# Diffusion block on one core: the first four token tiles of x loaded behind all sixteen pieces of the modulation weights

## The chip, the cores and the metric

The kernel runs on one core of one Trainium2 chip. The metric is the device time of one execution in microseconds (us). A difference of about 0.3% (4 us here) is what a measurement of this kernel can tell from no change.

## What is computed

One layer of a generator over 1024 latent tokens of width 1024, with 256 context tokens of the same width, all in float32:

```python
def layer(x, ctx, c, c_ctx, ...):
    sh1, sc1, gt1, sh2, sc2, gt2 = modulation(c, w_mod, b_mod)      # silu(c) @ w_mod + b_mod
    csh1, csc1, ... = modulation(c_ctx, w_mod, b_mod)
    hx = rms_norm(x, g_pre_mix) * (1 + sc1) + sh1
    hc = rms_norm(ctx, g_pre_mix) * (1 + csc1) + csh1
    s_f, s_b = context_states(hc, w_in, conv_qkv, a_log, dt_bias)    # K, V columns and gates only
    yx, _, _ = token_mixers(hx, rows, s_f, s_b, ...)                 # in-projection, short conv,
    x = x + gt1 * rms_norm(yx, g_post_mix)                           # gated delta rule, pooling, out-projection
    hx = rms_norm(x, g_pre_ffn) * (1 + sc2) + sh2
    x = x + gt2 * rms_norm(conv_glu_ffn(hx, w_up, conv_ffn, w_down), g_post_ffn)
```

The change lies in the first forty microseconds: the shift and scale of the modulation, the norms of x and of the context, and the loads behind them.

## The kernel before

**The start.** The modulation needs w_mod's first 2048 columns (the shift and the scale) before any token can be modulated. `stream_mod` loads them as sixteen pieces of 512 KB (tile `w_mod`, `NW` = 5 buffers), four pieces for each group of 512 columns in the order 2, 3, 0, 1, so that the scale comes first. Each piece takes four matmuls of 128x512 into `pa`. After the fourth piece of a group ScalarE copies the result (`rows`), and eight small matmuls turn it into columns (`m`); VectorE adds the bias (`mod`) and forms the scale `a`. When the last group is through, the event M1 lets the modulation of tokens begin. A piece's buffer is free for the piece five later once its matmuls are done.

**The token tiles.** x comes in eight tiles of 128 tokens, 512 KB each (tile `xv`, six buffers, shared with the two tiles of the context). Tiles 0 to 3 make up the half X0, tiles 4 to 7 the half X1. `XLOAD` says behind which piece of the modulation each of the first four is issued on SP's queue, which issues in order. Tiles 4 to 7 and the first pieces of w_in for the context (`w_c`, which use the buffers of `w_mod`) follow in the list `POST`.

**The chains.** For each set of tiles ScalarE takes the squares (`sq`), VectorE the reciprocal root in nine small steps (`ssq`, `rs_h`, `rs_a`, `rstd`), VectorE and POOL scale the tiles (`xv<-xv,rstd`), TensorE transposes them, and the result is copied to `xT_C` or `xT_X`. After M1 a unit of work for each of eight slices k makes `h` (VectorE; for X1 ScalarE straight from the transposes), rounds it to `c_hi` or `h_hi`, and takes the rest `c_lo` or `h_lo` (POOL for odd k, VectorE for even k). The products are made of three matmuls: hi by hi, lo by hi, hi by lo. The weights are split in the same way: `w_hi` by ScalarE, `w_lo` by POOL for the context, by VectorE for x.

**The jobs.** `gemm_T` runs 28 jobs, each 128 columns of w_in. Jobs 0 to 7 are those of the context (24 matmuls of 256 columns; four give `kc`, four `vc`). The job after them, job 8, is the first of x: two halves of 24 matmuls of 512 columns, the first of X0 and the second of X1. Each result (`rawc`, `raw`) goes through a short convolution of four VectorE steps for the context, of 128x256 each (on `kc`, `vc`), or four of 128x1024 for x (on `cv`). `gate_mm` makes the gates' columns, and `gate_tables` the tables for the context (`gtmp` of 128x16) and then for x (`gtmp` of 128x64): a row of some seventeen small VectorE steps, then three small matmuls `pb<-gtmp`. The rest of the modulation's weights comes in 32 pairs `w_m` with two buffers through `mod_rest`, between the jobs.

**What sets the order.** `Streams.run` picks the next step by priority and by a planner's clock (`Clock`), which gives each instruction a time of its own reckoning. Every engine then runs its own queue in that order. So a load that is issued later in the plan moves the work behind it on all engines. An instruction that waits in an engine's queue holds up all that stands behind it there.

The two places at which the table is used:

```python
NW, XLOAD = 5, (5, 7, 9, 11)
...
            wl.append(w)
            for t, n in enumerate(XLOAD):
                if n == i:
                    load_x(0, t)
                    signal(f"x{t}")
```

Of the kernel before, what the change touches and what calls it, by code (L numbers as in the profile page):

```python
# [28 lines left out]
GR = T // GW  # L29
EPS = 1e-6  # L30
NBIG, NK, NT4 = 9, 4, 2
NW, XLOAD = 5, (5, 7, 9, 11)
PT4 = (3,)
POST = [("w", 0)] + [("x", t) for t in range(4, 8)] + [("w", j) for j in range(1, 5)]

# [1925 lines left out]
```

## Time and profile before

| what | us |
|---|---|
| median of three runs (lowest, highest) | 1355.26 (1353.31, 1358.17) |
| the profiled execution | 1355.82 |
| its span, first to last instruction | 1354.1 |
| TensorE busy, of the span | 1268.3 |
| VectorE, ScalarE, POOL busy | 987.1, 632.8, 343.4 |
| stage from 630 us to the end: TensorE busy | 705.83 of 724 |

TensorE is busy through nearly all of the second half (the feed-forward part) and has its gaps before, most of them in the first 120 us. A busy time says nothing of a wait inside an instruction: a VectorE instruction that is held up by POOL is listed as busy. Times of the profile are counted from the span's start.

### The profile page before, as it was taken

How to read it: one execution, taken by the hardware profiler on the slowest of the kernel's cores; microseconds unless marked ns; L12 is line 12 of the kernel's file. 1: busy time of each engine (PE TensorE's matmuls, PEld its weight loads, DVE VectorE, ACT ScalarE, POOL GpSimd, SP SyncE). 2: the span in 40 equal slices, each digit the busy share in tenths (PEclk: the TensorE clock that was granted, in tenths of full speed). 3: DMA queues.
4: the chain of work that ended last, by engine and by line, in shares of the span. 5: the costliest groups of instructions: out<-in, count | busy, mean ns of one | idle time of the engine just before them, and what ended most of it. 6: DMA issues, size and time to landing. Idle time of an engine off the chain costs nothing.

```text
span 1354.1 us, 23855 instructions
## 1 busy us (share of the span) xinstructions
PE 1268.3 (94%) x8655; PEld 1003.1 (74%) x8655; DVE 987.1 (73%) x1917; ACT 632.8 (47%) x1502; POOL 343.4 (25%) x431
## 2 busy tenths in 40 slices
PE   5888989898999799988998999999999999999997
PEld 1456668686878678856876788888888887888886
DVE  1876655666778788447769999999877878765673
ACT  3555856355676435345544333333333335544541
POOL 0552334141141510003012334433333320000122
PEclk9989989999999889988999999999999999999999
DMA  9513655545562323375322566666334348976561
GB/s 349 196 40 106 201 167 140 173 123 169 147 188 80 75 78 96 105 253 173 138 83 88 196 241 233 240 237 233 137 116 140 126 138 282 308 235 194 190 215 62
DMA packets 145301, 226.54 MB, mean 167 GB/s; under 512 B 53440, under 2 KB 66592, under 8 KB 142368
## 3 DMA queue, kind: packets, MB, share of 16 engines
q1 hardware_dynamic: 144752, 224.61, 50.3%
q8 instruction: 68, 1.11, 0.3%
q10 hardware_dynamic: 432, 0.42, 0.1%
q14 instruction: 49, 0.40, 0.1%
HBM read 164.77 MB, written 60.21 MB: 166 GB/s over the span
## 4 chain that ended last, share of the span: by engine, by line
PE 73%; DVE 10%; DMA 8%; POOL 3%; ACT 3%; issue 2%; SPq 1%; DVEq 0%; POOLq 0%; ACTq 0%
PE pc L123 25%; PE pa L123 25%; PE pb L123 22%; DMA w_mod<-in_wmod 2%; POOL stmp L123 2%; POOL sX L123 1%; DVE hf L123 1%; DMA mx<-mixd 1%; DMA w_m<-in_wmod 1%; DVE gtmp L123 1%; DMA sc<-blk_x 1%; SPq L123 1%; DMA wo_st<-in_w_out 1%; DVE wql L123 1%; DMA sB<-blk_i 1%
## 5 line engine op out<-in xcount | busy, mean ns | idle before, releaser
L123 POOL TENSOR_TENSOR a<-a,a 128x512 f32<-128x512 f32 x88 | 149.7, 1702 | 315.6 <-DVE wql L123 142.3
L123 ACT CAST wqh<-a 128x512 fp32r<-128x512 f32 x132 | 80.8, 621 | 162.9 <-PE pb L123 73.3
L123 DVE TENSOR_TENSOR op<-dst,op 128x512 fp32r<-128x512 f32 x154 | 103.8, 714 | 57.4 <-ACT op L123 56.9
L123 PE MATMUL pa<-h_hi,w_hi 128*128 128x512 f32 x320 | 138.5, 433 | 2.5 <-ACT jk L123 1.2
L123 ACT CAST op<-dst 128x512 fp32r<-128x512 f32 x154 | 90.0, 620 | 93.8 <-PE pc L123 32.2
L123 PE MATMUL pa<-h_hi,w_lo 128*128 128x512 f32 x320 | 129.8, 406 | 1.6 <-DVE w_lo L123 1.6
L123 PE MATMUL pa<-h_lo,w_hi 128*128 128x512 f32 x320 | 130.1, 407 | 0.0
L123 PE MATMUL pc<-op 128*128 128x512 f32 x528 | 121.5, 390 | 0.0
L123 DVE TENSOR_TENSOR wql<-a,wqh 128x512 fp32r<-128x512 f32 x132 | 104.8, 796 | 18.4 <-ACT wqh L123 18.0
L123 PEld LDWEIGHTS pc<-op 128*128 128x128 f32 x528 | 99.0, 188 | 21.7 <-DVE graw L123 0.5
L123 DVE TENSOR_TENSOR hf<-hf 128x512 f32<-128x512 f32 (+1 forms) x109 | 92.0, 850 | 8.1 <-ACT hf L123 6.9
L123 POOL TENSOR_TENSOR hf<-hf,gg 128x512 f32<-128x512 f32 x16 | 21.3, 1350 | 214.5 <-ACT t L123 214.5
L123 PEld LDWEIGHTS pa<-h_hi,w_hi 128*128 128x128 f32 x320 | 61.2, 191 | 16.1 <-issue 2.8
L123 PEld LDWEIGHTS pa<-h_hi,w_lo 128*128 128x128 f32 x320 | 60.9, 190 | 13.9 <-DVE w_lo L123 1.8
L123 DVE SCALAR_TENSOR_TENSOR cv<-raw,sm,cv 128x1024 f32<-128x1024 f32 x48 | 62.5, 1301 | 11.4 <-ACT cv L123 10.8
L123 DVE SCALAR_TENSOR_TENSOR hf<-graw,sm,hf 128x1024 f32<-128x1024 f32 x44 | 70.0, 1590 | 0.7
L123 PEld LDWEIGHTS pa<-h_lo,w_hi 128*128 128x128 f32 x320 | 61.4, 192 | 9.6 <-issue 2.0
L123 ACT ACTIVATE hf<-hf 128x1024 f32<-128x1024 f32 x22 | 23.3, 1061 | 58.7 <-DVE hf L123 58.7
L123 PE MATMUL pa<-op 128*128 128x512 f32 x198 | 50.4, 390 | 0.0
L123 PE MATMUL pb<-op 128*128 128x512 f32 x198 | 50.3, 389 | 0.0
L123 ACT ACTIVATE ws<-pc,btg 128x128 f32<-128x128 f32 x80 | 26.8, 367 | 48.1 <-PE pc L123 47.7
L123 DVE TENSOR_TENSOR w_lo<-w_st,w_hi 128x512 fp32r<-128x512 f32 x40 | 28.4, 713 | 26.5 <-ACT w_hi L123 16.3
(388 smaller groups left out, 3328.0 us busy)
## 6 DMA issues: line engine op xcount, KB each, us to landing
a<-in_w_up_t SPq DMA_DIRECT2D x90, 256.0 KB, 3.2
w_m<-in_wmod SPq DMA_DIRECT2D x64, 256.0 KB, 3.2
hf<-in_w_down SPq DMA_DIRECT2D x22, 512.0 KB, 4.3
td<-hf SPq DMA_DIRECT2D x11, 1024.0 KB, 4.7
gd<-hf SPq DMA_DIRECT2D x22, 512.0 KB, 2.6
sd<-hf SPq DMA_DIRECT2D x11, 1024.0 KB, 5.4
dst<-sd SPq DMA_DIRECT2D x44, 256.0 KB, 4.7
dst<-td SPq DMA_DIRECT2D x44, 256.0 KB, 4.5
```

The lines of the kernel that those rows point to most:

```text
L123: return f(*a, **k)
```

## The change

The four numbers of `XLOAD` become 15 each: the loads of tiles 0 to 3 of x are issued behind the last of the sixteen pieces, all four together, instead of behind pieces 5, 7, 9 and 11.

```diff
-NW, XLOAD = 5, (5, 7, 9, 11)
+NW, XLOAD = 5, (15, 15, 15, 15)
```

**First place: the modulation.** SP's queue at the start, with the loads of the context's tiles, of w_mod's pieces and of x's tiles; before is -, now is +:

```order
 L123 DMA xv<-in_ctx 128x1024 x2
-L123 DMA w_mod<-in_wmod 128x1024 x6
-L123 DMA xv<-in_x 128x1024
-L123 DMA w_mod<-in_wmod 128x1024 x2
-L123 DMA xv<-in_x 128x1024
-L123 DMA w_mod<-in_wmod 128x1024 x2
-L123 DMA xv<-in_x 128x1024
-L123 DMA w_mod<-in_wmod 128x1024 x2
-L123 DMA xv<-in_x 128x1024
-L123 DMA w_mod<-in_wmod 128x1024 x4
+L123 DMA w_mod<-in_wmod 128x1024 x16
+L123 DMA xv<-in_x 128x1024 x4
```

The four tiles stand behind all pieces; ten loads of pieces move ahead of one or more of them. TensorE's queue from the last but one group of pieces to the context's gates (`pb<-cst,xv` are transposes of x's tiles):

```order
 L123 MATMUL m_186<-cst,rows 128x2 x4
-L123 MATMUL pa<-w_mod,cs 32x512 x4
-L123 MATMUL pb<-cst,xv 128x128 x6
-L123 MATMUL pa<-w_mod,cs 32x512 x2
-L123 MATMUL pb<-cst,xv 128x128 x2
-L123 MATMUL pa<-w_mod,cs 32x512 x2
-L123 MATMUL pb<-cst,xv 128x128 x5
+L123 MATMUL pa<-w_mod,cs 32x512 x8
 L123 MATMUL m_186<-cst,rows 128x2 x4
-L123 MATMUL pb<-cst,xv 128x128 x11
 L123 MATMUL pc<-c_hi_144,wg 32x256
 L123 MATMUL pc<-c_hi_145,wg 32x256
```

No transpose of x stands between the last pieces any more.

**Second place: x's first half behind the context.** POOL's queue (`c_lo` and `w_lo` belong to the context, `xv` to X0, `h_lo` to X0's slices):

```order
 L123 ISA
-L123 TENSOR_SCALAR xv<-xv,rstd 128x1024 x3
+L123 TENSOR_SCALAR xv<-xv,rstd 128x1024
+L123 TENSOR_TENSOR c_lo_153<-h_369,c_hi_145 128x256
+L123 TENSOR_TENSOR c_lo_155<-h_380,c_hi_147 128x256
+L123 TENSOR_TENSOR c_lo_157<-h_384,c_hi_149 128x256
+L123 TENSOR_TENSOR c_lo_159<-h_398,c_hi_151 128x256
+L123 TENSOR_TENSOR w_lo<-w_c,w_hi 128x512 x2
+L123 TENSOR_SCALAR xv<-xv,rstd 128x1024 x2
+L123 TENSOR_TENSOR w_lo<-w_c,w_hi 128x512 x6
+L123 TENSOR_TENSOR h_lo_128<-h_596,h_hi_120 128x512
```

POOL scales two tiles of X0 behind the context's four `c_lo` and job 0's two `w_lo`, and goes on with six `w_lo`. TensorE's queue in job 1, now:

```order
 L123 MATMUL pa<-c_hi_148,w_hi 128x256
 L123 MATMUL pa<-c_lo_156,w_hi 128x256
+L123 MATMUL pb<-gtmp_180,cst 128x8 x2
+L123 MATMUL pb<-gtmp_180,cst 128x16
+L123 MATMUL pb<-cst,xv 128x128 x4
+L123 MATMUL pa<-c_hi_148,w_lo 128x256
+L123 MATMUL pa<-c_hi_149,w_hi 128x256
+L123 MATMUL pa<-c_lo_157,w_hi 128x256
```

The first transposes of X0 stand behind the matmuls of the context's gate table.

**Third place: the gate tables of x.** TensorE's queue in job 8, before, where `pb<-gtmp_180` are the matmuls on that table:

```order
 L123 MATMUL pa<-c_hi_151,w_lo 128x256
-L123 MATMUL pa<-h_hi_119,w_hi 128x512
-L123 MATMUL pa<-h_lo_127,w_hi 128x512
-L123 MATMUL pa<-cst,kc 128x128 x3
-L123 MATMUL pa<-h_hi_119,w_lo 128x512
-L123 MATMUL pb<-gtmp_180,cst 128x32 x2
-L123 MATMUL pb<-gtmp_180,cst 128x64
```

They stand behind three matmuls of job 8's first half. Now, where `pa<-cst,kc` ends the first half:

```order
 L123 MATMUL pa<-cst,kc 128x128 x4
+L123 MATMUL pa<-h_hi_119,w_hi 128x512
+L123 MATMUL pa<-h_lo_127,w_hi 128x512
+L123 MATMUL pa<-h_hi_119,w_lo 128x512
+L123 MATMUL pa<-h_hi_120,w_hi 128x512
+L123 MATMUL pa<-h_lo_128,w_hi 128x512
+L123 MATMUL pa<-h_hi_120,w_lo 128x512
+L123 MATMUL pb<-gtmp_180,cst 128x32 x2
+L123 MATMUL pb<-gtmp_180,cst 128x64
```

Thirty matmuls of job 8, the first half and six of the second, stand ahead of the first matmul on x's gate table.

## Rows read from the trace of the kernel before

**Rows 1.** The page: busy us of each engine, share, instructions.

```profile
PE 1268.3 (94%) x8655; PEld 1003.1 (74%) x8655; DVE 987.1 (73%) x1917; ACT 632.8 (47%) x1502; POOL 343.4 (25%) x431
```

**Rows 2.** Stages: window, length, busy us of each engine, PEclk, DMA share, GB/s.

```profile
10.00:20.00 10.00, 9.73 (x46) 3.60 (x48) 4.05 (x17) 1.69 (x4) 1.60 (x1) 1.00 0.95 352
...
59.50:73.10 13.60, 7.57 (x35) 3.69 (x33) 13.40 (x40) 6.73 (x14) 8.40 (x6) 0.82 0.25 81
73.10:97.00 23.90, 20.32 (x117) 11.88 (x116) 19.74 (x31) 10.62 (x21) 17.67 (x13) 0.89 0.01 2
...
630.00:1354.00 724.00, 705.83 (x3087) 574.47 (x3085) 572.80 (x814) 290.28 (x522) 171.59 (x147) 1.00 0.53 182
```

**Rows 3.** Timeline, the end of the modulation: start, us, instruction, [idle before, releaser].

```profile
30.24 1.05 PE L123 MATMUL pa<-w_mod,cs 128*32 128x512 f32 x4 [0.17 <-DMA w_mod<-in_wmod]
...
34.01 0.14 PEld L123 LDWEIGHTS pa<-w_mod,cs 128*32 128x32 f32 x4 [0.91 <-DMA w_mod<-in_wmod]
...
38.21 1.92 PE L123 MATMUL pa<-w_mod,cs 128*32 128x512 f32 x4
...
40.69 1.19 PE L123 MATMUL pa<-w_mod,cs 128*32 128x512 f32 x4
...
43.65 0.17 DVE L123 TENSOR_TENSOR mod<-m,sm 128x16 f32<-128x16 f32 x1 [0.46 <-PE m L123]
```

**Rows 4.** Waits of SP's queue to 60 us: total us, times, longest.

```profile
SPq L123 <- PE pa L123: 9.6, 10, 2.0
```

**Rows 5.** Timeline, ScalarE and VectorE on X0 and the context.

```profile
27.82 1.06 ACT L123 ACTIVATE sq<-xv 128x1024 bf16<-128x1024 f32 x1 [2.31 <-DMA xv<-in_x]
...
33.00 0.17 DVE L123 TENSOR_SCALAR ssq<-ssq 128x4 f32<-128x4 f32 x1 [7.01 <-ACT sq L123]
...
40.58 0.69 DVE L123 COPY xT_X<-pb 128x512 f32<-128x512 f32 x1 [3.04 <-PE pb L123]
...
45.04 1.02 ACT L123 CAST c_hi<-h 128x256 fp32r<-128x256 f32 x3
```

**Rows 6.** Timeline of VectorE beside POOL's work.

```profile
55.31 0.55 DVE L123 TENSOR_SCALAR h<-xT_X,a,mod 128x512 f32<-128x512 f32 x1
...
63.55 1.29 DVE L123 TENSOR_TENSOR gtmp<-gtmp,gtmp 128x16 f32<-128x16 f32 x1
64.76 0.68 DVE L123 TENSOR_TENSOR h_lo<-h,h_hi 128x512 fp32r<-128x512 f32 x1
...
66.53 0.47 DVE L123 SCALAR_TENSOR_TENSOR kc<-rawc,sm,kc 128x256 f32<-128x256 f32 x1
...
72.87 0.16 DVE L123 SCALAR_TENSOR_TENSOR rstd<-rs_a,rstd 128x4 f32<-128x4 f32 x1
```

**Rows 7.** Timeline of POOL.

```profile
63.51 3.06 POOL L123 TENSOR_TENSOR w_lo<-w_c,w_hi 128x512 fp32r<-128x512 f32 x2 [0.17 <-ACT w_hi L123]
...
73.13 4.90 POOL L123 TENSOR_SCALAR xv<-xv,rstd 128x1024 f32<-128x1024 f32 x4 [1.20 <-DVE rstd L123]
...
94.44 1.45 POOL L123 TENSOR_TENSOR h_lo<-h,h_hi 128x512 fp32r<-128x512 f32 x1 [1.43 <-DVE h_hi L123]
```

**Rows 8.** Timelines of ScalarE and VectorE at x's gate table.

```profile
97.03 0.59 ACT L123 COPY gx<-pc 128x512 f32<-128x512 f32 x1 [4.47 <-PE pc L123]
...
114.33 0.21 DVE L123 TENSOR_TENSOR gtmp<-gtmp,gv 128x64 f32<-128x64 f32 x1
```

**Rows 9.** Timeline of TensorE: first and last matmul of job 8, a wait behind it.

```profile
110.10 0.40 PE L123 MATMUL pa<-h_hi,w_hi 128*128 128x512 f32 x1
...
130.59 0.39 PE L123 MATMUL pa<-h_hi,w_lo 128*128 128x512 f32 x1
...
137.96 0.43 PE L123 MATMUL pb<-w_m,cs 128*32 128x128 f32 x8 [0.59 <-DMA w_m<-in_wmod]
```

**Rows 10.** The page's DMA issues: count, KB, us from issue to landing.

```profile
w_m<-in_wmod SPq DMA_DIRECT2D x64, 256.0 KB, 3.2
```

## The prediction, made before the change was run

> **What bounds the kernel now.** I read the busy times first [rows 1]: TensorE works 1268 of 1354 us. The stages [rows 2] say where it doesn't: from 630 us on it is busy 705.8 of 724 us, so nothing at the start is worth anything there except by arriving sooner. From 59.5 to 73.1 us it works 7.6 of 13.6 us, VectorE 13.4. So the first 120 us are bound by VectorE and by POOL beside it, and the question is how soon TensorE can run the jobs of x. The first of these, job 8, begins at 110.1 and ends at 130.8 [rows 9]; behind it TensorE is nearly full. I take the end of job 8 as the mark: what the change moves there I carry to the end, since every later step hangs on earlier ones and not on a time of day.
>
> VectorE's prices, from starts of neighbouring rows (a row overlaps the next by some 0.08 us): `h` of 512 columns 0.46, `h_lo` 0.60, a convolution step 0.40, a copy `xT_X` 0.69, a small step 0.17 to 0.20 [rows 5, 6]. POOL's: `w_lo` 1.3 to 1.5, a tile `xv` 1.22, `h_lo` 1.45 [rows 7]. The two engines hinder each other: a `gtmp` step on 16 columns took 1.29 us beside a `w_lo` [rows 6, 7]. To price that I count VectorE's own work in a stage and ask which share of POOL's time is added. From 47.6 to 73.1 us VectorE had some 16.2 us of own work and POOL 15; the stage took 25.5, a share of 0.62. From 73.1 to 97.0 it had 10.9 (12 convolution steps, 8 roundings of about 0.36, 4 `h_lo`), POOL 17.7, and the stage took 23.9 [rows 2], a share of 0.7. These shares hold the waits for other engines too.
>
> **The change, step by step.**
>
> *M1 sooner.* Pieces 11 and 13 were used at 30.24 and 34.01 as they landed; between them came two pieces and a tile of x, 1.26 us each [rows 3]. Piece 15 would land at 34.0 + 2 x 1.26 = 36.5, but TensorE took pieces 14 and 15 at 38.21 and 40.69, since transposes of X0 stood ahead of them. With four loads of 512 KB taken out of the way piece 15 lands 4 x 1.26 = 5.0 us sooner, at 31.5 (30.6 at the 352 GB/s of 10 to 20 us [rows 2]), with no transposes between. From the last matmul to the end of `mod` is 43.84 - 40.69 = 3.2 us. M1 comes at 34.7 instead of 43.84: 9.1 us gained for the context. If it isn't the transfers that pace the pieces but SP's waits for buffers, 9.6 us in ten waits [rows 4], up to 4 us of this is lost.
>
> *X0's root later.* Tile 3 lands behind piece 15, at 31.5 + 5.0 = 36.5. ScalarE now has four `sq` (1.15 with the accumulator's read) and eight `c_hi` (0.35) in one queue [rows 5], 7.4 us from the first `h` at 35.05, with waits of some 0.5 for VectorE: X0's `ssq` comes at 42.9, against 33.0.
>
> *X0's transposes much later.* VectorE then has nine steps of the root (1.8), seventeen of the context's table (2.9), two tiles (1.5) and job 0's four convolution steps (1.6): 7.8 us. POOL has seven `w_lo` and two tiles, 11.7 us, times 0.62 is 7.3. That gives 58.0; TensorE takes the table's matmuls and, behind them, the first transposes of X0, with its clock likely low after the wait: 60.5, against 40.6 for the first copy before [rows 5]. This is the change's price, 20 us on X0, while job 0 and what hangs on it are sooner. The ends: 54 if the seventeen steps slip through between POOL's instructions, 65 if each of POOL's costs its full time.
>
> *X0's slices.* From 60.5: four copies (2.8), eight `h` (3.7), four `h_lo` (2.4), eight convolution steps (3.2), the root of X1 and small steps (2.9), 15.0 us; POOL five `w_lo` and four `h_lo`, 12.3 times 0.62 is 7.6. X1's root is ready at 83.1, against 73.0 [rows 6]. Tiles 6 and 7 wait for the buffers of tiles 0 and 1, so for X0's last transpose, near 72; they have 10 us for the load and two `sq`, which is enough but no more.
>
> *X1's slices.* Before, 73.0 to 95.9 (the last `h_lo` [rows 7]): 22.9 us with twelve convolution steps. Now again twelve, four of `kc` and eight of `vc`, and one `w_lo` less on POOL, 0.9: 22.0 us. X1 is ready at 105.1, 9.2 us later than before.
>
> *From X1 to the end of job 8.* Before, 130.8 - 95.9 = 34.9 us: four jobs of the context were still to come, with sixteen steps on `vc` and four `w_lo` of POOL, and x's gate table stood ahead of job 8. From the copy `gx` at 97.03 to the table's last product with `gv` at 114.5 [rows 8] went 17.5 us. Now eight steps on `vc` and all `w_lo` of the context are behind us: 17.5 less 4 x 1.4 x 0.7 = 3.9 and about 1 for a silu of `kc` that came earlier is 12.6, so the table is ready 1.1 + 12.6 = 13.7 us after X1. TensorE fills that time with 28 matmuls of the context (0.12 each) and 30 of job 8 (0.23), 10.3 us. It then has 18 matmuls (4.1) and three groups of `w_m` (1.4), and meets one wait for a pair of `w_m` of some 1.5 (a pair takes 3.2 us to land and has two buffers [rows 10]). Sum 20.7 us: job 8 ends at 125.8, 5.0 us sooner.
>
> *Behind job 8.* Two pairs of `w_m` now stand between jobs 9 and 10 with only twelve transposes and a few small matmuls between them, 2.4 us, against 3.2 for the landing: 0.8 us lost, of the kind of the 0.59 at 137.96 [rows 9].
>
> Sum: +9.2 at X1 (the 9.1 of M1 are already in it, eaten by X0's delay), -14.2 from there to the end of job 8, +0.8 behind it: -4.2 us. The profiled execution took 1355.82 us, 0.56 above the median of 1355.26; carried to the median the forecast is 1351.1.
>
> **The rivals.**
>
> *Slower: POOL holds VectorE for its full time.* The `gtmp` row of 1.29 us [rows 6] shows a small step that waited for all of a `w_lo`. If every instruction of POOL in the three stages costs VectorE its whole time, the shares 0.62 and 0.7 become 1: 0.38 x (11.7 + 12.3) + 0.3 x 16 = 13.9 us more, 1365. It decides from 4.2 us, a share of about 0.73 in all three. For it: POOL's work now comes in rows, nine instructions back to back behind the context; against: before had such rows too, and they are in the shares. The Trainium skill, "SBUF — State Buffer", section "Who interferes with whom", states that a VectorE instruction of this kind and a POOL instruction that reads the buffer exclude each other for the whole instruction; by that rule this rival's sum is the right one. The trace agrees for the `gtmp` row, but the shares over a stage are lower, since copies from PSUM and waits for others fall beside POOL's work.
>
> *No change: the lead on TensorE is given back.* VectorE's own queue (the last steps on `vc`, x's table) is through at about 118.8 now, and at about 119 before: nothing is gained there. If the heads' work behind job 8, VectorE's convolutions of 128x1024 and ScalarE's part, sets the pace, TensorE's 5 us are waited away: about 1355. The same comes out if the pieces are paced by buffers, so that the change moves the loads and not M1.
>
> *More gained:* the context's table slips through (54 instead of 60.5), X1 is ready at 98.6: 1344.6.
>
> **How the numbers follow.** Forecast 0.37, no change 0.30, slower 0.22, more gained 0.11. The forecast lies near the border of 0.3%, which is 4.1 us, about what a measurement can tell from no change; it is as likely above as below it in my working. So faster by over 0.3%: 0.11 + 0.37 x 0.7 + a share of the others = 0.40; within: 0.37; slower: 0.23. The range leaves out the full price of the lock and half of "more gained": 1345 to 1361.
>
> **What would show it.** `mod`'s last step near 34.5; X0's first `xT_X` copy near 60, between 54 and 65; X1's last `h_lo` near 105; job 8's end near 126. If the copy comes at 65 and X1 past 112, the lock's rival is right. If job 8 ends sooner by 5 us and the execution isn't shorter, the second is. Wrong would be above all the order of the three stages' prices, each a share taken from another mix of work.

## The result, and the profile after

The changed kernel took 1368.21 us, median of six runs (1366.57 to 1370.99); beside it the kernel before took 1356.72 (six runs, 1353.31 to 1361.26). The ratio is 1.0087, with a 95% interval of 1.0067 to 1.0107: slower by some 11.5 us, where 4 us faster was forecast, and outside the range (1345 to 1361). The profiled execution of after took 1370.99 us, its span 1369.3, so its own shift against [rows 1, 2]'s execution is 15.2 us, the largest of the six; the other five are 1.5 to 4.4 us shorter. The readings below are of that one execution.

The page, busy us of each engine, which answers [rows 1]:

```profile
PE 1272.3 (93%) x8655; PEld 1007.1 (74%) x8655; DVE 986.0 (72%) x1917; ACT 633.4 (46%) x1502; POOL 342.6 (25%) x431
```

The work is the same, TensorE 4 us busier (its mean granted clock was 0.969 of full speed, against 0.975). The end of the modulation, TensorE and VectorE, which answers [rows 3], then SP's queue (start, time from first to last issue):

```profile
33.78 1.91 PE L123 MATMUL pa<-w_mod,cs 128*32 128x512 f32 x12
36.16 1.05 PE L123 MATMUL pa<-w_mod,cs 128*32 128x512 f32 x4 [0.47 <-DMA w_mod<-in_wmod]
...
39.05 0.17 DVE L123 TENSOR_TENSOR mod<-m,sm 128x16 f32<-128x16 f32 x1 [14.31 <-PE m L123]
```

```profile
2.19 29.00 SPq L123 DMA_DIRECT2D w_mod<-in_wmod  x16
31.24 2.32 SPq L123 DMA_DIRECT2D xv<-in_x  x4
```

`mod` ends at 39.2, against 43.8 before and 34.7 forecast. The sixteen pieces take 29.0 us to be issued, and the transfers don't fill that time. Stages, with the same columns as [rows 2]; first 20 to 30 us after, then before:

```profile
20.00:30.00 10.00, 6.25 (x38) 2.21 (x36) 0.77 (x3) 0.96 (x2) 0.00 (x0) 0.95 0.83 267
```

```profile
20.00:30.00 10.00, 7.06 (x32) 1.73 (x31) 0.56 (x3) 4.22 (x8) 0.00 (x0) 1.00 1.02 413
```

267 GB/s where before moved 413: with no tile between them, the pieces wait for their buffers (the second experiment takes that wait away). Next X0 behind the context, VectorE, then POOL, which answer [rows 5 to 7]:

```profile
47.01 0.17 DVE L123 TENSOR_SCALAR ssq<-ssq 128x4 f32<-128x4 f32 x1 [1.19 <-ACT sq L123]
...
57.15 3.64 DVE L123 SCALAR_TENSOR_TENSOR gtmp<-gtmp,gtmp 128x16 f32<-128x16 f32 x3
...
65.74 0.69 DVE L123 COPY xT_X<-pb 128x512 f32<-128x512 f32 x1 [0.76 <-PE pb L123]
```

```profile
54.58 6.18 POOL L123 TENSOR_TENSOR w_lo<-w_c,w_hi 128x512 fp32r<-128x512 f32 x5
...
113.22 1.45 POOL L123 TENSOR_TENSOR h_lo<-h,h_hi 128x512 fp32r<-128x512 f32 x1 [0.96 <-DVE h_hi L123]
```

Beside five `w_lo` in a row (1.24 us each) three `gtmp` steps take 1.21 us each: one small step per POOL instruction, where such a step alone takes 0.17. X0's first copy comes at 65.74, X1's last `h_lo` ends at 114.67 (95.89 before). Then x's gate table and TensorE around jobs 8 to 10, which answer [rows 8, 9]:

```profile
126.81 0.22 DVE L123 TENSOR_TENSOR gtmp<-gtmp,gv 128x64 f32<-128x64 f32 x1
```

```profile
119.93 0.39 PE L123 MATMUL pa<-h_hi,w_hi 128*128 128x512 f32 x1
...
133.40 0.40 PE L123 MATMUL pa<-h_hi,w_lo 128*128 128x512 f32 x1
...
149.77 0.42 PE L123 MATMUL pb<-w_m,cs 128*32 128x128 f32 x8 [0.58 <-DMA w_m<-in_wmod]
...
151.98 0.42 PE L123 MATMUL pb<-w_m,cs 128*32 128x128 f32 x8 [0.73 <-DMA w_m<-in_wmod]
...
155.05 0.44 PE L123 MATMUL pb<-w_m,cs 128*32 128x128 f32 x8 [1.79 <-DMA w_m<-in_wmod]
...
158.55 2.08 PE L123 MATMUL pb<-kc 128*128 128x128 f32 x8 [1.67 <-DVE N L123]
...
162.13 0.48 PE L123 MATMUL pa<-h_hi,w_hi 128*128 128x512 f32 x1
```

Job 8 begins at 119.93 and ends at 133.80, only 2.8 us later than before (130.98): the 30 matmuls that run ahead of the gate table are there as the order said. Job 9 ends at 150.6 (148.2 before). But the first matmul of job 10 comes at 162.13, against 151.04 before. Before, the last of the small products `pb<-kc` and that matmul:

```profile
146.41 1.05 PE L123 MATMUL pb<-kc 128*128 128x128 f32 x8
...
151.04 0.50 PE L123 MATMUL pa<-h_hi,w_hi 128*128 128x512 f32 x1 [1.15 <-ACT jk L123]
```

The way from the end of job 8 to job 10, which I had put down with 0.8 us more, takes 28.33 us instead of 20.06. TensorE's groups in that stretch (busy, mean ns of one, idle before), after and then before:

```profile
L123 PE MATMUL pb<-w_m,cs 128*32 128x128 f32 x80 | 4.5, 312 | 4.3 <-DMA w_m<-in_wmod 4.3
L123 PE MATMUL pb<-kc 128*128 128x128 f32 x16 | 3.8, 393 | 1.7 <-DVE N L123 1.7
```

```profile
L123 PE MATMUL pb<-w_m,cs 128*32 128x128 f32 x64 | 3.2, 283 | 0.6 <-DMA w_m<-in_wmod 0.6
L123 PE MATMUL pb<-kc 128*128 128x128 f32 x16 | 2.5, 287 | 0.0
```

There are waits for `w_m` of 4.3 us instead of 0.6; a wait of 1.7 for N, a table of the context's state, that before doesn't have; one group of `w_m` more on this side of the mark; and slower instructions: in 150 to 160 us TensorE was busy 5.82 of 10 us and its granted clock was 0.77 of full speed, between the levels of 1.2 and 2.4 GHz. The chain of waits of after runs through this place:

```profile
145.82 3.90 DMA w_m<-in_wmod
149.77 0.47 PE pb L123 x8
150.26 4.75 DMA w_m<-in_wmod
155.05 1.18 PE pb L123 x10
156.34 2.17 DVE N L123 x8
158.55 2.09 PE pb L123 x8
...
160.94 0.87 DVE N L123 x3
...
167.79 3.69 DMA sB<-blk_i
```

With the last of the eight products the chain leaves TensorE: it goes on over N on VectorE, N's blocks that SP sends to memory and back (`sB`), and the state's solve on POOL to the first products behind the solve, after and then before:

```profile
193.76 1.07 PE L123 MATMUL pb<-sc,N 32*32 32x32 f32 x64 [2.47 <-DMA sc<-blk_x]
```

```profile
180.46 0.85 PE L123 MATMUL pb<-sc,N 32*32 32x32 f32 x64
```

The last product `pb<-kc` ends at 160.63 instead of 147.46, 13.2 us later, and `pb<-sc` comes 13.3 us later: this row carries the shift, and the first matmul of job 10 (11.1 us later) only stands near it. The second half takes what it took before (706.20 busy of its last 724 us, against 705.83 in [rows 2]).

The reason for the new stretch is in TensorE's queue. Before, the eight products `pb<-kc`, which make N, stand within job 9, four behind its 29th and four behind its 45th matmul; now all eight stand behind its 48th and last, among the groups of `w_m`, with no matmul of x left to cover a landing. The planner didn't ask for this: from ahead of job 8 on it writes the same sequence for both kernels. So an engine's queue isn't quite the planner's order: the build orders each queue once more by its own reckoning of when operands are ready, and that came out differently.

### The profile page after: what moved, and what is told of

The parts are those of the page before. It is cut to its first block, busy times and chain, and to the rows that moved or that the text cites. A ratio compares the mean times of both kernels' runs of the same rounds, so it can differ in the third digit from the quotient of the medians.

```text
span 1369.3 us, 23859 instructions
## 1 busy us (share of the span) xinstructions
PE 1272.3 (93%) x8655; PEld 1007.1 (74%) x8655; DVE 986.0 (72%) x1917; ACT 633.4 (46%) x1502; POOL 342.6 (25%) x431
## 4 chain that ended last, share of the span: by engine, by line
PE 74%; DVE 9%; DMA 8%; POOL 3%; ACT 2%; issue 2%; SPq 1%; DVEq 0%; POOLq 0%; ACTq 0%
PE pa L123 26%; PE pc L123 26%; PE pb L123 22%; DMA w_m<-in_wmod 2%; POOL stmp L123 2%; DMA w_mod<-in_wmod 1%; POOL sX L123 1%; DVE hf L123 1%; DMA sc<-blk_x 1%; DMA wo_st<-in_w_out 1%; SPq L123 1%; DVE wql L123 1%; DMA sB<-blk_i 1%; DMA mx<-mixd 1%; DVE gtmp L123 1%
## 5 line engine op out<-in xcount | busy, mean ns | idle before, releaser
L123 DVE TENSOR_TENSOR wql<-a,wqh 128x512 fp32r<-128x512 f32 x132 | 103.5, 787 | 17.9 <-ACT wqh L123 17.6
L123 PEld LDWEIGHTS pc<-op 128*128 128x128 f32 x528 | 99.1, 188 | 21.6 <-DVE graw L123 0.5
L123 DVE TENSOR_TENSOR w_lo<-w_st,w_hi 128x512 fp32r<-128x512 f32 x40 | 27.8, 696 | 26.1 <-ACT w_hi L123 23.8
```

The lines of the kernel that those rows point to most:

```text
L123: return f(*a, **k)
```

## Experiments

In most of these kernels every engine's queue is held word for word in a given order, by an edge without a wait between neighbours, so that one thing changes at a time:

```python
def _pin(tc):
    order = json.loads(zlib.decompress(base64.b85decode(ORD)))
    ...
        for a, b in zip(q, q[1:]):
            tc.add_manual_dep(b, a.name, mybir.DependencyInfo(mybir.DependencyClass.NoSync, ...))
```

"Order of after" and "order of before" mean this below; no run holds the order of after and changes nothing else. The median of before shifted by up to 2.4 us between the chips, so each result has its ratio to the runs of before beside it, and differences between kernels are taken from the ratios, at 13.6 us for 0.01: after itself, at 1.0087, is 11.8 us slower than before.

**The loads alone.** Order of after, the four tiles issued behind pieces 5, 7, 9, 11:

```diff
-L123 DMA w_mod<-in_wmod 128x1024 x16
-L123 DMA xv<-in_x 128x1024 x4
+L123 DMA w_mod<-in_wmod 128x1024 x6
+L123 DMA xv<-in_x 128x1024
...
```

> Every engine's queue stands in the order of the changed kernel, word for word; only the four loads of x's first tiles go out behind pieces 5, 7, 9 and 11 again, as before. If the loss comes from the late landing of the four tiles, it goes away: about 1357 us. If it comes from the order in which the engines' queues now stand, it stays, 1366 to 1370, and with the four loads among the pieces again M1 falls back towards 43 and the time may be up to 4 us worse than the changed kernel: up to 1373. I expect the second: X0's four squares stand behind the roundings of the context on ScalarE in this order, so an early tile only waits longer.

1369.91 us, 1.0118 (1.0094 to 1.0142). The loss stays (16 us; the intervals of the two overlap), so the landing of the tiles isn't its cause. But M1 didn't go back to 43:

```profile
38.85 0.17 DVE L123 TENSOR_TENSOR mod<-m,sm 128x16 f32<-128x16 f32 x1 [13.40 <-PE m L123]
46.81 0.17 DVE L123 TENSOR_SCALAR ssq<-ssq 128x4 f32<-128x4 f32 x1 [1.19 <-ACT sq L123]
```

Both are within 0.2 us of after. So four loads of 512 KB among the pieces cost M1 nothing, and what gained 4.6 us there came with the order of the queues. In it no transposes of X0, which wait for X0's root, stand between the last pieces on TensorE; that these are the whole of it isn't shown.

**The buffers of the pieces.** Pieces 5 to 15 each land in a buffer of its own, in memory that the slices of x use later; order of after, then order of before.

```diff
+    stage = [hp.tile([P, 2, 512], F32, name="stage", tag="h", bufs=2 * KT) for _ in range(11)]
...
-            w = xp.tile([P, 2, 512], F32, name="w_mod", tag="w_mod", bufs=NW)
...
+                w = stage[i - NW]
```

> The changed kernel in its own order, but pieces 5 to 15 of the modulation's weights land in buffers of their own (in the place that the slices of x take later), so that no load waits for a buffer. If buffers paced the pieces, piece 15 lands near 31.5 and M1 comes at 34 to 36 instead of 39.2; if it is the transfers, M1 stays within 1 us of 39.2. The four tiles of x land sooner by the same. If the start of the context sets the rest, the whole time falls by 4 to 5 us, to about 1364; if the queues of VectorE and POOL behind M1 swallow it, it stays at 1368.

> The kernel before in its own order, with pieces 5 to 15 in buffers of their own. If the buffers paced its pieces too, M1 comes at 38 to 41 instead of 43.84 and the time falls by 2 to 4 us, to 1352 to 1354. If TensorE's queue (the transposes of X0, which stand between the last pieces and wait for X0's root) sets M1 there, M1 stays at 43 to 44 and the time within 1 us of before.

After with its own buffers: 1364.01 us, 1.0062 (1.0033 to 1.0092), 3.4 us less than after, though the intervals overlap; M1, SP and the rate, from this run:

```profile
32.54 0.17 DVE L141 TENSOR_TENSOR mod<-m,sm 128x16 f32<-128x16 f32 x1 [8.04 <-PE m L141]
```

```profile
7.75 11.99 SPq L376 DMA_DIRECT2D stage<-in_wmod  x11
```

```profile
20.00:30.00 10.00, 8.49 (x62) 3.62 (x63) 0.78 (x3) 1.55 (x3) 0.00 (x0) 1.00 1.03 412
```

The buffers pace the pieces: 412 GB/s again, M1 at 32.7, 6.5 us sooner. In the profiled executions all of this reaches the end (7.0 us), by the ratios half; how much it is can't be told. Before with its own buffers: M1 at 40.0 instead of 43.8, and 1353.53 us, 0.9993 (0.9975 to 1.0011), no difference that can be told. The transposes still stand between the last pieces there, but they come sooner themselves, since X0's root does (30.7 instead of 33.0).

**POOL's share.** The sixteen `w_lo` of the context left out of POOL (the jobs' third product takes `w_hi` a second time), in the order of after and of before.

```diff
-                yield from split_steps(whi, wlo, w, *(SPLITS[m] if i < NCJ else (V,)))
...
+                    S.copy(whi, w)
```

> The changed kernel in its own order without POOL's sixteen w_lo of the context's weights (that part is left out: the third product of the context's jobs takes w_hi a second time, so TensorE's work is the same). If POOL's rows of w_lo hold VectorE in the stretch behind the context, the first copy xT_X comes at 57 to 60 instead of 65.7, X1's last h_lo near 103 instead of 113.2, and the time falls by 9 us or more, to 1359 or below. If POOL costs VectorE little there, the time stays above 1364.

> The kernel before in its own order, with the same sixteen w_lo of POOL left out. If POOL's rows are what makes the change slower, the two kernels without them come out alike (within 4 us), so this one gains much less than the changed kernel does. If the order of the queues is the cause, the difference of 11 us stays between the two kernels without w_lo.

1352.37 us, 0.9972 (0.9951 to 0.9993), and 1339.04 us, 0.9902 (0.9868 to 0.9935). After gains 15.6 us, before 13.3 (8.8 to 17.9 by its interval), and they stay 9.5 apart. X1's last `h_lo` comes 15.6 us sooner in after (99.1) and 11.8 in before (84.1). In after X0's first copy comes at 58.53 and the small steps take 0.2 us:

```profile
54.06 0.60 DVE L141 SCALAR_TENSOR_TENSOR gtmp<-gtmp,gtmp 128x16 f32<-128x16 f32 x3
```

So POOL does hold VectorE, and dearly: the sixteen are 20.7 us of POOL's time in after and 22.2 in before, and by the medians 0.75 and 0.60 of it are paid for by the whole (0.56 to 0.95 and 0.40 to 0.81 by the intervals). But before pays nearly as much: by the medians 2 of the 11.8 us may come from POOL's rows, by the intervals anything from nothing to 8, and the last of the eight products ends 16.2 us sooner in after and 16.4 in before.

**The order behind job 8.** Order of after up to the end of job 8, of before from job 9 on; then the same with the pieces' own buffers. In TensorE's queue, within job 9:

```diff
 L123 MATMUL pa<-h_hi_120,w_hi 128x512
 L123 MATMUL pa<-h_lo_128,w_hi 128x512
+L123 MATMUL pb<-w_m_1348,cs 32x128 x4
+L123 MATMUL pb<-kc 128x128 x2
+L123 MATMUL pb<-w_m_1350,cs 32x128 x4
+L123 MATMUL pb<-kc 128x128 x2
```

> The changed kernel in its own order up to the end of job 8; from job 9 on every engine's queue stands as in the kernel before (there the eight products kc for the context's state stand within job 9, four behind its 29th and four behind its 45th matmul, where the changed kernel has all eight behind the job's last). If the second part of the loss, 8.6 us between the end of job 9 and the first matmul of job 10, is made by that order, job 10 begins 3 to 4 us behind job 9 and the time falls to 1359 to 1361. If the products would wait anyway (the state's N comes late whatever the order), job 9 is stretched instead and the time stays above 1365.

> Both at once in the changed kernel: pieces 5 to 15 in buffers of their own, and the order of before from job 9 on. If the two losses are separate, their gains add (4.2 and about 8 us): 1355 to 1357, level with the kernel before or 1 us above. If a lead gained at the start is waited away behind job 8, no more than the larger of the two: 1360.

1366.52 us, 1.0093 (1.0068 to 1.0118): nothing gained, against the expectation. The way from job 8 to job 10 is 26.4 us; N no longer waits, but `w_m` still does (2.0 us) and TensorE's granted clock was 0.87 of full speed:

```profile
136.01:162.41 26.40, 22.76 (x162) 15.22 (x162) 14.65 (x43) 17.14 (x63) 3.88 (x3) 0.87 0.68 218
```

With both: 1356.44, 1.0020 (1.0002 to 1.0037), 9.1 us less than after, where the two alone gave 3.4 and nothing. Each of these differences is known to 4 or 5 us only, so it isn't shown that the pair gives more than its parts. The way was 25.9 us in that run too.

**Half the change.** Planned and built afresh:

```diff
-NW, XLOAD = 5, (15, 15, 15, 15)
+NW, XLOAD = 5, (9, 11, 13, 15)
```

> Half the change: the four tiles behind pieces 9, 11, 13 and 15, with the order that follows from it (the eight products kc stand behind the last matmul of job 9, as in the changed kernel). If the loss behind job 9 goes with that order, this kernel has it too, about 8 us, and X0's transposes near 55 to 60: 1362 to 1368. If the loss grows with the delay of the tiles alone, half of it, 1361.

1371.18, 1.0131 (1.0103 to 1.0158): no better than the whole, and above the 1362 to 1368 expected. X0's first copy came at 55.41, ten us sooner than in after, and x's gate table at 129.0, two later. The loss doesn't follow the delay of the tiles.

**What holds the groups of `w_m`.** The copy of x's gate table to memory moved from SP's queue to ScalarE's, order of after; then the same with the pieces' own buffers in the order of before.

```diff
-        dma(out=gd.rearrange("c (t p) -> (c t) p", p=P), in_=gts[:m])
...
+            nc.scalar.dma_start(out=gd_to, in_=gts[:m])
```

> The changed kernel in its own order; one transfer is moved from SP's queue to ScalarE's: the copy of x's gate table to memory (gdram). On SP it goes out at 130.93, and the third pair of w_m at 132.15 and the two loads of N for the context's state stand behind it. If SP's queue behind the late gate table is what TensorE pays for between jobs 8 and 10, the pair goes out 8 us or more sooner and the time falls by 3 to 6 us, to 1362 to 1365. If the pair waits for its buffers anyway (the matmuls on the second pair stand on TensorE behind the table's own matmuls, at 131.67), it goes out at 131 to 132 as before and the time stays within 2 us of 1368.

> A version that might beat both: the kernel before in its own order, with pieces 5 to 15 of the modulation's weights in buffers of their own and the copy of x's gate table on ScalarE's queue. The buffers alone gave 1353.5 against 1355.25. If M1 3.8 us sooner is carried to the end, 1350 to 1352; if it is given back in the stretch that ScalarE, VectorE and POOL bound, 1354 to 1356.

1366.07 us, 1.0068 (1.0047 to 1.0088), 2.6 us less than after, and the intervals overlap; the pair goes out at 131.46 (132.15 in after), just as much sooner as the gate table of that run was ready, so SP's queue isn't the holder. The pair waits for its two buffers, whose matmuls stand on TensorE behind those on the gate table. The second kernel: 1353.88, 0.9985 (0.9970 to 0.9999), 2 us faster than before if anything, and not to be told from the buffers alone (0.9993).

Then the loads of `w_m` taken away behind the first pair (all 32 groups of matmuls use it, so the rest of the modulation isn't computed), in the order of after and of before:

```diff
             for m in range(2):
...
-                dma(out=ws[m], in_=I["wmod2"][j, :, 4 * m:4 * m + 4, :])
...
+                if j == 0:
...
+                    nc.sync.dma_start(out=w0[m], in_=I["wmod2"][j, :, 4 * m:4 * m + 4, :])
```

> The changed kernel in its own order without the loads of w_m behind the first pair (left out: all 32 groups of matmuls use the first pair, so TensorE's work is the same, and no group waits for a landing). If the landings of w_m take back TensorE's lead behind job 8, the way from the end of job 8 to the first matmul of job 10 falls from 28.3 us to 22 or less and the time by 5 to 8 us against the changed kernel. If the context's state (N) or the clock does it, the way stays above 25 us and the time falls by less than 3.

> The kernel before in its own order, with the same loads left out. In it one wait of 0.59 us for w_m stands between jobs 8 and 10, so by the theory of the landings the kernel before gains 1 to 3 us only, and the two kernels without the loads lie 5 to 8 us apart instead of 13. If w_m is not the cause, they lie 11 to 13 us apart as before.

1362.97 us, 1.0038 (1.0023 to 1.0054), and 1354.44, 0.9979 (0.9965 to 0.9993): 8.0 us apart instead of 11.8. The way in after is 24.5 us, between the 22 and the 25 of the two cases expected, and the wait for N has grown into the gap:

```profile
L141 PE MATMUL pb<-cst,mrow 128*128 128x128 f32 x4 | 1.2, 292 | 2.4 <-DVE N L141 2.4
```

Loading N earlier on SP, beside that, changed nothing. SP's queue:

```diff
 L123 DMA gdram<-gtmp_182 64x128
+L123 DMA N<-gcdram 128x1024 x2
```

> The changed kernel in its own order, without the loads of w_m behind the first pair (left out, as above) and with the first two loads of N, for the context's state, moved on SP's queue from behind the third and fourth pair of w_m to right behind the copy of x's gate table. If what stays of the long way from job 8 to job 10 (24.5 us without the loads of w_m, against 20.1 in the kernel before) is the wait for N (2.4 us) that follows from SP's order, the way falls to 21 or 22 us and the time to 1358 to 1361. If N waits for ScalarE's and TensorE's queues in this order, the way stays at 24 to 25 us and the time at 1362 to 1364.

1360.11, 1.0039 (1.0018 to 1.0059); the wait for N stays at 2.42 us. So it isn't for N's load; that it is for N's place in the queues is argued and not shown. Last, the landings of `w_m` and the order behind job 8 together:

> The changed kernel without the loads of w_m behind the first pair (left out, as above) and with every queue from job 9 on in the order of the kernel before. Alone, the first took the way from the end of job 8 to the first matmul of job 10 from 28.3 to 24.5 us, the second to 26.4. If the landings of w_m and the place of the eight products kc are the two parts of the 8.3 us, the way is now 20 to 21 us, as in the kernel before, and the time lies 5 to 7 us below the changed kernel's 1368 plus what job 10 gains: 1358 to 1361. If a third thing (the late gate table and what is computed from it) holds TensorE, the way stays at 23 us or more.

1356.25 us, 1.0000 (0.9985 to 1.0016): level with the kernel before, and 2.8 us above before without those loads. The way is 22.25 us, at full clock and without a wait for a landing or for N:

```profile
135.09:157.34 22.25, 19.97 (x161) 13.57 (x162) 15.46 (x43) 17.09 (x63) 4.19 (x3) 1.00 0.44 142
```

The time fell further than expected (1358 to 1361), the way less far (20 to 21). So the landings of `w_m` and the order behind job 8 make up some 9 of the 11.8 us. That order is the one of every engine's queue from job 9 on; no run moves the eight products alone.

**The row that carries the time.** The profiled executions of these kernels, by the end of job 8 and the end of the last product `pb<-kc` (us, counted in the span):

| kernel | end of job 8 | from there to the last product's end | from there to the end |
|---|---|---|---|
| before | 130.98 | 16.5 | 1206.6 |
| after | 133.80 | 26.8 | 1208.7 |
| after, order of before behind job 8 | 136.01 | 22.8 | 1207.4 |
| after, without the loads of `w_m` | 132.86 | 23.0 | 1205.9 |
| after, both | 135.09 | 18.7 | 1202.8 |

In the eleven kernels that stand in one of the two orders, or in one up to job 8 and the other behind it, and load all of `w_m`, the last column is 1205.4 to 1208.7, while their spans go from 1336.8 to 1369.3: when the last of the eight products ends, the time is all but settled. The change adds 10.3 us between job 8 and that row; the order alone takes back 4.0, the landings alone 3.9, both 8.2. That the order alone shows no gain in its ratio fits with job 8 itself, which ended 2.2 us later in that execution: M1, ahead of all that the edit moves, came at 40.5 instead of 39.2 (38.6 to 40.6 in the eight kernels with after's order there and five buffers; why it varies isn't shown). With own buffers the order is worth nearly the same: 22.4 us instead of 26.1.

**Is there something faster than both?** `w_lo` of the context on VectorE (planned and built afresh from before), half of them, and all with the pieces' own buffers:

```diff
-    SPLITS = ((G, S.copy), (G, S.copy))
+    SPLITS = ((V, S.copy), (V, S.copy))
```

> A version that might beat both: the kernel before with the sixteen w_lo of the context's weights on VectorE instead of POOL (order as it follows). Leaving POOL's sixteen w_lo out was worth 16 us in both kernels; on VectorE they take 0.6 to 0.69 us each, some 10.4 us. If POOL's instructions hold VectorE as long as measured, the net is 5 us faster, 1350; if VectorE is the bound there and POOL's work lay mostly beside it, 5 us slower or more, 1360.

> The same with eight of the sixteen w_lo on VectorE and eight left on POOL: half the effect of the whole, 1352 to 1353, if the two are additive; better than the whole, below 1350, if the two engines work best side by side.

> All w_lo of the context on VectorE, and pieces 5 to 15 of the modulation's weights in buffers of their own: 2 to 4 us below the kernel with w_lo on VectorE alone if M1 still sets the start of that stretch; no better if not.

1349.53 us, 0.9952 (0.9936 to 0.9968); 1363.80, 1.0062 (1.0045 to 1.0078); 1346.72, 0.9942 (0.9917 to 0.9968). The whole move is faster than before by 6.5 us (5.6 expected from 16 less 10.4; VectorE's sixteen took 10.9, 681 ns each):

```profile
L123 DVE TENSOR_TENSOR w_lo<-w_c,w_hi 128x512 fp32r<-128x512 f32 x16 | 10.9, 681 | 0.2 <-ACT w_hi L123 0.2
```

The number agrees, but the mechanism isn't shown by it: in the profiled execution (1354.23) job 8 ended at 119.63, 11.4 us sooner than before, X1's last `h_lo` came at 97.0 (95.9) and `pb<-sc` at 184.55 (180.46), so what was gained lies behind that. Half the move is slower than before by 8.4 us, where some 4 us faster was expected, and no price of an instruction explains it: `pb<-sc` came at 179.22, 1.2 us sooner than before, and the loss lies behind it. Each of the three has an order of its own. Whether the buffers add to the whole move can't be told (the intervals overlap).

## Why the prediction was wrong, step by step

- *M1 sooner*: 39.2, not 34.7; 4.6 us gained, not 9.1. The step counted transfers. The caveat that it carried was the truth: the pieces are paced by five buffers (29.0 us of issuing, 267 GB/s; with own buffers 32.7). And what was gained came with the order of the queues, in which no transposes stand between the last pieces, not from the four loads taken out of the way, which are worth nothing there (first experiment).
- *X0's root later*: 47.0, not 42.9, which is the 4.5 us of M1; counted from M1 it is 7.8 us, as in the working (8.2).
- *X0's transposes*, *X0's slices*, *X1's slices*: 65.74 - 39.22 = 26.5 from M1 (25.8 forecast), 24.4 to X1's root (22.6), 24.5 for X1's slices (22.0). Together 5.0 us more than the sums. Their kind was right, their share of POOL seems small: 0.75 as measured in after by leaving out `w_lo`, instead of 0.62 and 0.7. With it the three sums grow by 0.13 x (11.7 + 12.3) + 0.05 x 16 = 3.9 us; but that 0.75 is known to 0.56 to 0.95 only, so this part is argued. The shares were also misread: POOL worked 16.2 us from 47.6 to 73.1, not 15, which gives 0.57, and 13.0 of 17.7 is 0.73, not 0.7. Together that moves the forecast by half a microsecond. X1 is ready at 114.7 instead of 105.1: 4.5 from M1, 5.0 from here.
- *From X1 to the end of job 8*: 133.8 - 114.7 = 19.1 us, 20.7 forecast. Near enough, and so job 8 ended 2.8 us late although X1 came 18.8 late.
- *Behind job 8*: this term failed. 0.8 us forecast, 28.33 - 20.06 = 8.3 measured up to job 10, and 10.3 up to the last of the eight products. TensorE's lead over the gate table was given back: the groups of `w_m` stand behind the matmuls on that table, two buffers let only one pair land at a time, and the eight products that used to stand within job 9 now stand behind it, where nothing covers a landing. I had looked at one pair of landings (2.4 against 3.2 us) and not at what else of the queue had moved past job 9. The mark was wrong with it: in after the chain of waits passes by the end of job 8 (it goes over a landing of `w_m` from 132.15 to 134.82) and runs through the state's products. "Every later step hangs on earlier ones" was true, but not on this one.

The errors of size (4.5 and 5.0 at X1, -1.6 to job 8, 7.5 behind it) are 15.4 us between the forecast's -4.2 and the profiled job 10's +11.1; the last products, at +13.2, lie another 2 us off. The chances don't agree with their own words either: 0.7 of the forecast's 0.37 went to "faster by over 0.3%", though the text calls both sides of that border equally likely.

Of the rivals, *POOL holds VectorE* gave the nearest time, 1365, and its sign was met (the copy at 65.74, X1 at 114.7), mostly by luck: 4.5 us of both are M1's, its price is real, but the kernel before pays nearly the same. The Trainium skill, "SBUF — State Buffer", section "Who interferes with whom", states that a VectorE instruction with two inputs in this buffer and a POOL instruction that reads the buffer exclude each other; the rows of three `gtmp` steps at 1.21 us beside `w_lo` agree with it. Leaving POOL's work out shows that by the medians 0.60 to 0.75 of its time is paid. *The lead is given back* named the right kind, but VectorE's and ScalarE's convolutions as the place; the place was the landings of `w_m` and the products `kc`, and it gave back more than the lead.

What stays open: the last 2.2 us from job 8 to the last product (18.7 against 16.5), what moving the eight products alone would give back, and how much of the 5.0 us at X1 is POOL's.

## What to carry to other kernels

When a change re-plans the queues, follow every instruction that changes its place up to where the two orders run together again, and not to the first convenient mark: a mark is only good if the chain of waits runs through it. Here that was the end of eight small products, 2.5 us of work, and not the end of a big job. A lead that one engine gains by running other work ahead is given back at the first row that still hangs on the late thing, here small groups with two buffers behind a late table. And a stream that is "paced by transfers" should first be asked for its rate: here 267 GB/s beside 413 was the sign that buffers paced it.

## What the hardware showed

- VectorE's small steps beside a row of POOL's two-input work advance one per POOL instruction (1.21 us instead of 0.17). Of the 21 to 22 us that sixteen such instructions take on POOL, 0.60 to 0.75 by the medians (0.4 to 0.95 by the intervals) were paid for by the whole kernel; the same sixteen on VectorE take 10.9 us.
- From 20 to 30 us, loads of 512 KB with five buffers moved 267 GB/s, with eleven more buffers 412, the same as with other loads among them (413 in the kernel before).
- In a stretch in which TensorE was busy 5.82 of 10 us (150 to 160) the granted clock was 0.77, and the products `pb<-kc` took 393 ns each instead of 287 at a clock of 1.00 before, about 1.3 us on top of the waits themselves.
